# Decoder trunk on one core: weight halves kept in DRAM for the even layer only

## The chip, the cores and the metric

One Trainium2 chip, one of its cores. The metric is the time on the device of one launch, in microseconds (us). The kernel before took 2595.64 us in the median of three runs (2592.78 to 2598.08).

## The reference, cut to what matters

A hybrid decoder trunk takes one step for 1024 prompt tokens and 8 sample tokens, 1032 columns in all, with a model width of 1024 and everything in float32. It has two layers.

- Layer 0 (even) is an RMSNorm, one input projection of 1024 x 2560, sliding-window attention beside an RWKV-7 recurrence, an output projection, and a ConvFFN.
- Layer 1 (odd) is an RMSNorm, a gated chunk mixer, and a second ConvFFN. The mixer is `z = gelu(x W)`, split into u and v; v gets a LayerNorm and is mixed over chunks of 128 tokens; then `(u * mixed) W_out`.
- Each ConvFFN is `gelu(conv3(x W_gate)) * (x W_up)`, then `W_down`, with 2816 = 22 x 128 inner columns.

A float32 product is made of three matmuls: every operand is split into a high part `hi` (rounded to the float32r type) and a rest `lo = x - hi`, and `hi*hi + hi*lo + lo*hi` is summed (`mm3`, L288).

## The kernel before, in words

Activations lie transposed, 128 features on the partitions and tokens along the row. After the even mixer the 1032 tokens are in two halves (`HALVES`, L780): hA is chunk 0 with 512 tokens, and hB is chunks 1 and 2 with 256 and 264.

Weights come in slabs, 128 output columns by 1024 inputs. A global list `order` (L177 to L191) names every slab in the order of use. `wget` (L275) hands out the next slab and sees that the following ones are loaded, `LOOK2` = 3 slabs ahead in the layers' later parts. `wload` (L235) does the loading. From index `wfirst` on, the first slab of `gate0`, it counts as `late`. For each half j (128 x 512) of a slab:

- on the first visit, the raw half goes into a `raw` tile (a ring of `NRAW` = 3) by a DMA of 256 KB on SP's queue (L259); ACT copies it into `hi` (L285), and POOL computes `lo` (L286; for a few slabs it is DVE);
- if the slab will be asked for again (`more`), both parts are stored to DRAM as `wk`, 256 KB each, again on SP's queue (L263);
- on a later visit (`again`), both parts are loaded from there straight into the `w` tiles (L254), and nothing is split.

The `w` tiles are a ring of 18 in the late part (8 with tag `w`, 10 with tag `w2`), so four and a half slabs fit.

Late slabs that are asked for twice, once for hA and once for hB: gate and up, f = 0 to 7 in layer 0 and f = 0 to 5 in layer 1 (`gate_up`, L560); the last eight `down` slabs of either layer (`down`, L710, four slabs to a step: two steps for hA, then two for hB); and all slabs of `win_odd` and `wout_odd` (`odd_mix`, L1619). These are 24 + 20 + 24 = 68 slabs. The remaining gate and up slabs go through `pair` (L677), which builds combinations of weights (`wa`, `ws`) and touches each slab once. The even layer asks for each of its 28 slabs four times.

Around the gate and up steps of hB stands `combos` (L593): it loads the activations again (`ta`, `yA`, `yB` from `xnd`, L599) and forms differences of them on DVE, with splits on ACT, DVE and POOL, for the pairs that follow.

SP issues nearly all DMAs, in order. Engines work in program order; which order that is, a list scheduler decides at build time from simulated times and priorities. So the order in time differs from the order of the code.

Of the kernel before, what the change touches and what calls it, by code (L numbers as in the profile page):

```python
# [123 lines left out]
def trunk(ctx: ExitStack, tc: tile.TileContext, A, O):  # L124
# [12 lines left out]
    def nm(s):  # L137
        uid[0] += 1
        return f"{s}_{uid[0]}"
# [18 lines left out]
    def dram(shape, s, dt=F32):  # L158
        return dp.tile(shape, dt, tag=s, name=s)
# [17 lines left out]
    order = []  # L177
# [22 lines left out]
    def wtile(late):  # L200
        if late:
            wcount[0] += 1
        if late and (wcount[0] <= 4 * W2ONLY or wcount[0] % (NW + FBUFS["w2"]) >= NW):
            return wmore[0]("w2", 512, F32R)
        return wp.tile([P, 512], F32R, tag="w", name=nm("w"))
# [3 lines left out]
    def wfactor(name, f, i):  # L209

        if i == 0:
            wraw[name, f] = [stile("wa")[:, 0:512] for _ in range(4)]
            for k, t in enumerate(wraw[name, f]):
                SP.dma_start(out=t, in_=A[name][f + k // 2][:, k % 2 * 512:k % 2 * 512 + 512])
        r = wraw[name, f]
        if i == 0:
            return r[0]
        if i == 1:
            r.append(stile("ws", "g")[:, 0:512])
            DVE.tensor_tensor(out=r[4], in0=r[2], in1=r[3], op=ALU.add)  # L220
            return r[4]
        if i == 2:
            DVE.tensor_tensor(out=r[4], in0=r[4], in1=r[0], op=ALU.subtract)
            return r[4]
        if i == 3:
            return r[1]
        if i == 4:
            DVE.tensor_tensor(out=r[2], in0=r[0], in1=r[2], op=ALU.subtract)
            return r[2]
        if i == 5:  # L230
            DVE.tensor_tensor(out=r[4], in0=r[1], in1=r[4], op=ALU.subtract)
            return r[4]
        return r[3]

    def wload(i):  # L235


        late = i >= wfirst
        if late:
            look[0] = LOOK3 if len(order[i]) == 3 else LOOK2  # L240
        if len(order[i]) == 3:
            hi, lo = wtile(late), wtile(late)
            split(wfactor(*order[i]), hi, lo, POOL)
            wtiles[i] = tuple([x[:, k * P:(k + 1) * P] for k in range(4)] for x in (hi, lo))
            return
        name, m = order[i]
        again = order.index((name, m)) < i
        more = order.count((name, m)) > 1
        hi, lo = [], []
        for j in range(2):  # L250
            t = [wtile(late) for _ in range(2)]
            if again:
                for part in range(2):
                    SP.dma_start(out=t[part].bitcast(F32), in_=wkept[name, m, j, part])  # L254
                hi.append(t[0])
                lo.append(t[1])
                continue
            raw = wp.tile([P, 512], F32, tag="raw", name=nm("raw"), bufs=NRAW)
            SP.dma_start(out=raw, in_=A[name][m][:, j * 512:j * 512 + 512])  # L259
            split(raw, *t, DVE if SW[0] <= i - wfirst < SW[1] and i % SW[2] == 0 or i < SW[3] else POOL)  # L260
            for part in range(2 if more else 0):
                kept = wkept[name, m, j, part] = dram([P, 512], nm("wk"))
                SP.dma_start(out=kept, in_=t[part].bitcast(F32))  # L263
            hi.append(t[0])
            lo.append(t[1])
        wtiles[i] = ([hi[k // 4][:, (k % 4) * P:(k % 4 + 1) * P] for k in range(KD)],
                     [lo[k // 4][:, (k % 4) * P:(k % 4 + 1) * P] for k in range(KD)])
# [7 lines left out]
    def wget(*key):  # L275
        i = wpos[0]
        wpos[0] += 1
        assert order[i] == key, (order[i], key)
        while wnext[0] <= min(i + look[0], len(order) - 1):
            wload(wnext[0])  # L280
            wnext[0] += 1
        return wtiles.pop(i)

    def split(src, hi, lo, eng=None):
        ACT.activation(out=hi, in_=src, func=AF.Copy)  # L285
        (eng or DVE).tensor_tensor(out=lo, in0=src, in1=hi.bitcast(F32), op=ALU.subtract)  # L286
# [1533 lines left out]
```

## Time and profile before

| | us |
|---|---|
| median of 3 runs | 2595.64 |
| the profiled execution's own time | 2596.03 |
| its span (first to last instruction) | 2594.2 |

A profile's page lists the busy time of each engine over the span, the same in 40 slices, the DMA queues, the chain of work that ended last, the costliest groups of instructions, and the DMA issues with their time from issue to landing. PE is the matmul engine, ACT and DVE and POOL work on rows of 128 partitions, SP issues DMAs. "Idle before" an instruction is the time in which its engine stood still, and the releaser is what it waited for. In the table of windows each row is one stretch of the span, with the busy time of each engine, the granted clock of PE, the busy share of the DMA engines and the GB/s that they moved.

In the span, layer 0's gate and up steps begin in earnest at about 742 us, hB's at about 864 us; its last down steps are at 1440 to 1516 us. The odd mixer is at about 1520 to 1830 us, layer 1's gate and up steps follow to 1987 us, and its last down steps are at 2495 to 2566 us.

### The profile page before, as it was taken

The numbers are of one execution on the slowest core, as the hardware profiler recorded it, in microseconds if no ns is written. First come the engines' busy times: TensorE is split into PE (matmuls) and PEld (weight loads), VectorE is DVE, ScalarE is ACT, GpSimd is POOL, SyncE is SP. The second block draws the span as 40 slices with busy tenths as digits, with TensorE's granted clock in tenths as the row PEclk, the third lists the DMA queues.
The fourth block names the chain that finished last, engine by engine and source line by source line (L and its number), as shares of the span: only waits on it lengthen the run. The fifth ranks groups of instructions, "written<-read, shape, count | busy, mean of one in ns | idle before, by whom it ended". The sixth has DMA issues, their size and how long they took to land.

```text
span 2594.2 us, 49897 instructions
## 1 busy us (share of the span) xinstructions
PE 2450.8 (94%) x18508; PEld 2263.8 (87%) x18508; DVE 1600.0 (62%) x3471; ACT 982.8 (38%) x1937; POOL 863.2 (33%) x943
## 2 busy tenths in 40 slices
PE   6799998999889799999999899998999999999996
PEld 5688887888777699999999787988889999998986
DVE  5776859656864636766455476345576766655545
ACT  4444535434343334444411244443544444441110
POOL 1601113110434215555322344211534555542221
PEclk9889999998799899999999999999999999999998
DMA  8777657765499962223646789565995233264585
GB/s 310 269 235 215 212 182 239 239 220 161 157 328 326 351 227 99 98 103 123 227 132 211 280 271 314 185 207 162 329 357 201 97 105 120 85 208 147 187 282 167
DMA packets 330069, 542.89 MB, mean 209 GB/s; under 512 B 52769, under 2 KB 96353, under 8 KB 329825
## 3 DMA queue, kind: packets, MB, share of 16 engines
q1 hardware_dynamic: 329824, 539.70, 61.9%
q8 instruction: 145, 2.38, 0.4%
q14 instruction: 100, 0.81, 0.1%
HBM read 353.93 MB, written 183.00 MB: 207 GB/s over the span
## 4 chain that ended last, share of the span: by engine, by line
PE 77%; DVE 9%; DMA 6%; issue 3%; POOL 2%; ACT 2%; SPq 1%; DVEq 0%; POOLq 0%; ACTq 0%
PE l L289 17%; PE l L290 17%; PE l L291 17%; PE le L291 3%; PE le L289 3%; PE le L290 3%; PE m L291 2%; PE m L289 2%; PE m L290 2%; DMA w<-wk 2%; POOL w L286 1%; PE ch L1490 1%; PE ch L1493 1%; DMA raw<-in_win_even_dram 1%; PE pr L1380 1%
## 5 line engine op out<-in xcount | busy, mean ns | idle before, releaser
L286 POOL TENSOR_TENSOR w<-raw,w 128x512 fp32r<-128x512 f32 x228 | 310.8, 1373 | 603.1 <-ACT w L285 546.6
L289 PE MATMUL l<-xB,w 128*128 128x256 f32 (+2 forms) x1072 | 303.2, 286 | 18.7 <-DMA w<-wk 10.2
L285 ACT ACTIVATE w<-raw 128x512 fp32r<-128x512 f32 x248 | 153.4, 628 | 417.6 <-PE l L290 257.0
L289 PE MATMUL l<-xA,w 128*128 128x258 f32 (+1 forms) x896 | 301.8, 337 | 6.5 <-ACT w L285 5.9
L291 PE MATMUL l<-xA,w 128*128 128x258 f32 (+1 forms) x896 | 301.9, 337 | 3.5 <-POOL w L286 3.3
L291 PE MATMUL l<-xB,w 128*128 128x264 f32 (+2 forms) x1072 | 305.2, 286 | 0.0
L290 PE MATMUL l<-xB,w 128*128 128x264 f32 (+2 forms) x1072 | 304.8, 285 | 0.0
L290 PE MATMUL l<-xA,w 128*128 128x258 f32 (+1 forms) x896 | 301.6, 337 | 0.6 <-DVE xA L286 0.6
L289 PE MATMUL le<-xs,w 128*128 128x256 f32 (+1 forms) x896 | 270.1, 302 | 25.3 <-ACT w L285 19.5
L291 PE MATMUL le<-xs,w 128*128 128x256 f32 (+1 forms) x896 | 268.0, 300 | 9.7 <-POOL w L286 6.3
L290 PE MATMUL le<-xs,w 128*128 128x256 f32 (+1 forms) x896 | 265.3, 296 | 0.6 <-DVE xs L286 0.6
L289 PEld LDWEIGHTS l<-xB,w 128*128 128x128 f32 x1072 | 203.0, 191 | 20.5 <-ACT yA L285 10.6
L286 POOL TENSOR_TENSOR w<-wa,w 128x512 fp32r<-128x512 f32 x120 | 187.8, 1571 | 74.2 <-ACT w L285 65.4
L289 PEld LDWEIGHTS le<-xs,w 128*128 128x128 f32 x896 | 178.1, 199 | 37.9 <-ACT w L285 22.4
L290 PEld LDWEIGHTS l<-xB,w 128*128 128x128 f32 x1072 | 204.4, 191 | 0.2
L291 PEld LDWEIGHTS l<-xB,w 128*128 128x128 f32 x1072 | 204.1, 190 | 0.1
L291 PEld LDWEIGHTS le<-xs,w 128*128 128x128 f32 x896 | 177.6, 199 | 17.7 <-POOL w L286 8.1
L289 PEld LDWEIGHTS l<-xA,w 128*128 128x128 f32 x896 | 169.6, 189 | 25.6 <-ACT w L285 7.4
L291 PEld LDWEIGHTS l<-xA,w 128*128 128x128 f32 x896 | 169.5, 189 | 22.5 <-POOL w L286 4.6
L290 PEld LDWEIGHTS l<-xA,w 128*128 128x128 f32 x896 | 169.4, 189 | 18.0 <-DVE xA L286 0.7
L290 PEld LDWEIGHTS le<-xs,w 128*128 128x128 f32 x896 | 178.3, 199 | 4.6 <-issue 2.1
L725 DVE TENSOR_TENSOR yA<-yA,l 128x512 f32<-128x512 f32 x128 | 87.5, 687 | 149.7 <-PE l L291 149.7
(484 smaller groups left out, 6635.4 us busy)
## 6 DMA issues: line engine op xcount, KB each, us to landing
w<-wk SPq DMA_DIRECT2D x608, 256.0 KB, 4.1
wk<-w SPq DMA_DIRECT2D x384, 256.0 KB, 3.7
raw<-in_down_dram SPq DMA_DIRECT2D x88, 256.0 KB, 5.3
ta<-hd SPq DMA_DIRECT2D x36, 512.0 KB, 4.6
hd<-cb SPq DMA_DIRECT2D x30, 516.0 KB, 4.0
hd<-ub SPq DMA_DIRECT2D x30, 516.0 KB, 3.9
wa<-in_gate_dram SPq DMA_DIRECT2D x60, 256.0 KB, 2.9
wa<-in_up_dram SPq DMA_DIRECT2D x60, 256.0 KB, 2.6
```

Of the source, the lines that this page charges most:

```text
L285: ACT.activation(out=hi, in_=src, func=AF.Copy)
L286: (eng or DVE).tensor_tensor(out=lo, in0=src, in1=hi.bitcast(F32), op=ALU.subtract)
L289: PE.matmul(out, wh, xh, start=start, stop=False, **kw)
L290: PE.matmul(out, wh, xl, start=False, stop=False, **kw)
L291: return PE.matmul(out, wl, xh, start=False, stop=stop, **kw)
L725: DVE.tensor_tensor(out=yc, in0=yc, in1=ps[:, :n], op=ALU.add)
L1380: PE.matmul(pa[:, hp * 128:(hp + 1) * 128], BK[hp][s, e * 128:(e + 1) * 128], KR[hp][s, e * 128:(e + 1) * 128], start=True, stop=True)
L1490: PE.matmul(ps[:, hp * 128:(hp + 1) * 128], KR[hp][:, e * 128:(e + 1) * 128], Tc[:, hp * 128:(hp + 1) * 128], start=(hp == 0), stop=False, ...
L1493: PE.matmul(ps[r0:r0 + 64, h * 64:(h + 1) * 64], Av[e][:, h, r0:r0 + 64], UV[e][:, h * 64:(h + 1) * 64], start=False, stop=(h % 2 == 1), s ...
```

## The change

`again` and `more` are false for every late slab. The even layer goes on as before. Each late slab that is asked for twice is loaded raw and split on both visits, and is not stored in between.

```diff
         name, m = order[i]
-        again = order.index((name, m)) < i
-        more = order.count((name, m)) > 1
+        again = not late and order.index((name, m)) < i
+        more = not late and order.count((name, m)) > 1
         hi, lo = [], []
```

With 68 slabs of two halves and two parts, 272 stores `wk<-w` and 272 loads `w<-wk` go. In their place come 136 loads `raw<-in_...`, 136 ACT copies and 136 subtractions on POOL.

## Rows read from the trace of the kernel before

**Rows 1.** The page, busy time of the engines: us, share of the span, instructions.

```profile
PE 2450.8 (94%) x18508; PEld 2263.8 (87%) x18508; DVE 1600.0 (62%) x3471; ACT 982.8 (38%) x1937; POOL 863.2 (33%) x943
```

**Rows 2.** The page, the span in 40 slices, the busy share of each in tenths.

```profile
PE   6799998999889799999999899998999999999996
...
DMA  8777657765499962223646789565995233264585
```

**Rows 3.** The page, costliest groups: the split of raw halves on POOL and on ACT. After the bar: busy us, mean ns of one, idle before.

```profile
L286 POOL TENSOR_TENSOR w<-raw,w 128x512 fp32r<-128x512 f32 x228 | 310.8, 1373 | 603.1 <-ACT w L285 546.6
...
L285 ACT ACTIVATE w<-raw 128x512 fp32r<-128x512 f32 x248 | 153.4, 628 | 417.6 <-PE l L290 257.0
```

**Rows 4.** DMA issues over the whole span: count, KB each, median us from issue to landing.

```profile
w<-wk SPq DMA_DIRECT2D x608, 256.0 KB, 4.1
wk<-w SPq DMA_DIRECT2D x384, 256.0 KB, 3.7
raw<-in_down_dram SPq DMA_DIRECT2D x88, 256.0 KB, 5.3
...
raw<-in_gate_dram SPq DMA_DIRECT2D x28, 256.0 KB, 4.2
```

**Rows 5.** The table of windows: length, then PE, PEld, DVE, ACT and POOL busy with the number of instructions, PE's granted clock, DMA share, GB/s.

```profile
742.00:864.00 122.00, 109.47 (x539) 89.32 (x537) 69.64 (x123) 46.65 (x82) 52.94 (x56) 0.97 0.93 325
864.00:882.00 18.00, 5.51 (x27) 5.16 (x27) 13.16 (x13) 7.31 (x12) 6.27 (x6) 0.70 1.06 395
882.00:920.00 38.00, 35.33 (x283) 35.12 (x283) 20.04 (x34) 12.45 (x26) 5.67 (x8) 0.96 0.97 333
...
1840.00:1900.00 60.00, 60.00 (x292) 49.73 (x292) 43.73 (x85) 31.36 (x53) 38.23 (x41) 1.00 0.95 327
1440.00:1516.00 76.00, 65.96 (x421) 60.03 (x420) 47.17 (x96) 20.03 (x32) 17.88 (x13) 0.93 0.82 291
2495.00:2566.00 71.00, 65.78 (x426) 60.60 (x425) 31.92 (x68) 7.91 (x13) 6.57 (x7) 0.93 0.74 256
1620.00:1680.00 60.00, 60.00 (x494) 59.25 (x492) 23.08 (x34) 24.64 (x47) 9.34 (x8) 1.00 0.53 175
```

**Rows 6.** The timeline of PE: start us, us, instruction, and in brackets the idle time before it with its releaser.

```profile
831.36 0.50 PE L291 MATMUL l<-xA,w 128*128 128x512 f32 x1 [1.96 <-POOL w L286]
...
874.27 0.55 PE L289 MATMUL l<-xB,w 128*128 128x256 f32 x1 [10.16 <-DMA w<-wk]
...
906.06 0.39 PE L289 MATMUL l<-xB,w 128*128 128x256 f32 x1 [2.67 <-DVE gb L588]
...
1451.43 0.79 PE L289 MATMUL l<-gb,w 128*128 128x512 f32 x1 [3.72 <-ACT w L285]
...
1477.56 0.74 PE L291 MATMUL l<-cb,w 128*128 128x256 f32 x4 [3.57 <-DMA w<-wk]
...
2552.84 0.36 PE L289 MATMUL l<-gb,w 128*128 128x256 f32 x1 [1.77 <-DMA w<-wk]
```

**Rows 7.** The chain that ended last, in order of time: start us, us, what.

```profile
852.47 7.14 DMA wk<-w
...
859.68 5.24 DMA wk<-w
...
864.94 6.62 DMA yB<-xnd
...
1443.66 7.01 DMA raw<-in_down_dram
```

**Rows 8.** DMA issues of two stretches alone, 760 to 870 us (first row) and 1620 to 1690 us (second row): count, KB each, median us to landing.

```profile
wk<-w SPq DMA_DIRECT2D x50, 256.0 KB, 4.3
...
wk<-w SPq DMA_DIRECT2D x22, 256.0 KB, 2.4
```

**Rows 9.** The timelines of POOL (first row) and DVE at 897 to 903 us.

```profile
899.44 3.00 POOL L286 TENSOR_TENSOR yB<-t,yB 128x516 fp32r<-128x516 f32 x2
...
897.99 0.22 DVE L546 SCALAR_TENSOR_TENSOR gb<-st,vec,gb 128x8 f32<-128x8 f32 x1
...
899.27 0.75 DVE L543 SCALAR_TENSOR_TENSOR cb<-cb,vec 128x512 f32<-128x512 f32 x1
899.94 1.27 DVE L546 SCALAR_TENSOR_TENSOR cb<-st,vec,cb 128x8 f32<-128x8 f32 x1
901.13 1.86 DVE L543 SCALAR_TENSOR_TENSOR gb<-gb,vec 128x512 f32<-128x512 f32 x1
```

**Rows 10.** DVE at 900 to 1000 us, one group: the product that empties a PSUM bank in `gate_up`.

```profile
L588 DVE TENSOR_TENSOR cb<-cb,l 128x256 f32<-128x256 f32 x4 | 1.7, 418 | 0.8 <-ACT cb L586 0.8
```

## The prediction

> **What bounds the kernel now.** I read the busy times first: PE is busy 94% of the span, DVE 62, ACT 38, POOL 33 [rows 1]. PE bounds the whole, and an edit that changes no matmul can only give back or take PE's idle time and its lost clock. The slices (64.9 us each) then show where the DMA engines are full: the 12th to 14th (713 to 908 us), the 24th and 25th, the 29th and 30th and the 39th have 8 or 9 tenths. PE falls to 7 tenths in the 14th and to 8 in the 23rd, and keeps its 9 in the 29th and 30th [rows 2]. So I took windows of the late part [rows 5]. Idle time of PE is the length less its busy time: 12.5 us in hA's gate and up steps of layer 0 (742 to 864), 12.5 in the 18 us after them, 2.7 in 882 to 920, 10.0 in layer 0's last down steps, 5.2 in layer 1's. Two windows have none: 1840 to 1900, hA's gate and up of layer 1, and 1620 to 1680, in the odd mixer. The first of these is a warning: loads, splits and stores run there as at 742 to 864, the DMA engines are 0.95 busy, and PE stands still for 0.00 us. Full DMA engines alone cost nothing; it needs something that waits for one transfer.
>
> The timeline gives those places [rows 6]: 10.16 us at 874 on a load `w<-wk`, 3.72 at 1451 on an ACT split, 3.57 at 1477 and 1.77 at 2552 on `w<-wk`, 1.96 at 831 on a POOL split, 2.67 at 906 on DVE. The chain in order of time tells what is behind the first: two stores `wk<-w`, 7.14 and 5.24 us, stand on it one after the other, and only then the load `yB<-xnd` of 6.62 us whose data DVE needs before it comes to xB [rows 7]. And the ACT split at 1451 stood behind a raw load that took 7.01 us to land [rows 7], where the median over the span is 5.3 [rows 4].
>
> **The change part by part.** It takes 272 of 384 stores and 272 of 608 reloads out [rows 4] and puts 136 raw loads in: 408 transfers of 256 KB fewer, 107 MB. It adds 136 ACT copies of 0.628 us, 85 us, and 136 POOL subtractions of 1.373 us, 187 us [rows 3]. Spread over the span that takes POOL from 33% to 40% and ACT from 38% to 41%. Both have room; the question is place.
>
> *Second visits in general.* A slab of hB is 48 matmuls. At 60 us for 494 of them [rows 5] that is 5.8 us, against 2.7 us of POOL and 1.3 us of ACT for its two halves. Supply of raw halves: a ring of three, each held for its landing (4.2 us), ACT (0.63) and POOL (1.37), together 6.2 us [rows 3, 4]; so a half every 2.1 us and a slab every 4.1, under 5.8. The cover is PE's own work on a slab. If a landing took 7.01 us [rows 7] it would be 9.0 us for three, 6.0 per slab, and PE would wait 0.2 us per slab. In the odd mixer I therefore cost the second visits at 0; there is no idle time to win there. Bounds: 0 and +5 (two stalls as at 906).
>
> *hA of layer 0, 742 to 864.* 64 stores (16.8 MB of the 39.6 MB that 325 GB/s move in 122 us [rows 5]) go. Landings should fall from 4.3 us towards the 2.4 of a window at half the load [rows 8]. The order of the engines stays about the same, and 1840 to 1900 shows that such a stretch need not wait for stores at all. I take 3 of the 12.5 us: the 1.96 at 831 and about half as much elsewhere. Bounds: -12.5 and +3 (a changed order).
>
> *The start of hB, 864 to 882.* The two stores on the chain are 12.4 us [rows 7]. In place of one of them a raw load of 4.2 us [rows 4] may stand, so the load of `yB` comes some 8.2 us earlier. After that, while only hB's first chunk is there, PE needs a slab in 24 matmuls (2.9 us) and the raw ring gives one in 4.1: 1.2 us late per slab, for two slabs 2.4. The clock is 0.70 here for 5.51 us of matmuls [rows 5]; without the long stall 1.7 us of that comes back. Sum: -8.2 + 2.4 - 1.7 = -7.5. Bounds: -14.2 (all idle time and all of the clock), and +5 (four slabs late, no gain).
>
> *DVE and POOL side by side, in hB of both layers.* Here 32 and 24 subtractions come to POOL that were not there. What they do to DVE can be seen at 899 to 903 us [rows 9]: L546 takes 0.22 us alone and 1.27 while POOL subtracts, L543 0.75 and 1.86. The two POOL instructions cost DVE 2.2 us, and PE's wait of 2.67 us at 906 for L588 follows upon it [rows 6]. DVE is busy 33.2 of 56 us here [rows 5], so about every second new subtraction meets it. PE only feels it when four PSUM banks are full (4 x 2.9 = 11.6 us of cover). I take one more such wait, +2.7. Bounds: -2.7 (the wait at 906 goes, since `combos` starts earlier) and +21 (four in each layer).
>
> The Trainium skill has a rule for this, in "SBUF — State Buffer", section "Who interferes with whom": a DVE instruction with two inputs in SBUF and a GpSimd instruction that reads SBUF exclude each other for the whole instruction. The trace agrees in kind: L546 and L543, with two such inputs, are held, while L588, with one input in PSUM, keeps a mean of 418 ns [rows 10]. By the rule every meeting costs DVE up to a whole subtraction, and the sum below would be the second rival's.
>
> *Last down steps.* Four slabs to a step leave 2 of 18 `w` tiles over, so most of the next step's halves can only be split when the last matmuls of a step release tiles. For a step of hB I estimate what PE waits as 6.2 us (landing, ACT, POOL) less 2.9 us of matmuls on the halves already there: 3.3 us, twice per layer, 6.6. In layer 0 the two reload waits and what goes with them are 10.0 - 3.72 = 6.3 us now [rows 5, 6]: +0.3. The 3.72 at 1451 shrinks by 7.01 - 4.2 = 2.8. Of the clock (0.93 on 66 us, 4.6 us) I take 0.5 back. Sum -3.0; bounds -14.6 and +6 (landings of 7.01 us: 2 x 6.1 - 6.3). In layer 1 it is 6.6 against 5.2 us now: +1.4; bounds -9.8 and +7.
>
> *SP.* Its queue has 408 issues fewer. A raw load may hold it until a raw tile is free, as a reload held it until a `w` tile was free; I cost this at nothing, since the DMAs behind are the same.
>
> Sum: 0 - 3 - 7.5 + 2.7 - 3.0 + 1.4 = -9.4 us. Against the profiled execution's 2596.03 us that is 2586.6; its time is 0.4 us above the median of the runs, which is nothing here. I predict 2587.
>
> **The rivals.**
> 1. *Everything that waits for a weight transfer goes.* For it: 10.16 + 3.72 + 3.57 + 1.77 + 1.96 us of waits are weight waits [rows 6], and some 6 us of clock go with them: -27, 2569. Against it: in the down steps tiles, not transfers, are short.
> 2. *POOL holds DVE: slower.* In the stretches where `combos` runs, about 39 us in layer 0 and 24 in layer 1, two subtractions come per 5.8 us, 22 in all. If each two of them cost PE what the two at 899 did, that is 11 x 2.67 = 29 us, against 12 us of gains: +17, 2613. It decides once DVE's queue is more than 11.6 us behind, so that all four banks wait. For it: 2.67 us at 906 [rows 6, 9]. Against: in 1840 to 1900 POOL is busy 38 and DVE 44 of 60 us, and PE never waits [rows 5].
> 3. *The raw ring is too short in the down steps.* With landings of 7 us, +13 in both layers, and no more than 5 won elsewhere: 2604.
> 4. *Hidden anyway.* The stall at 874 is replaced by another of the same length, since hB's start hangs on the norm before it and its round trip through DRAM: 2595, within 3. For it: the 0.00 us at 1840 to 1900 in spite of a DMA share of 0.95 [rows 5].
>
> That the change does not do what it says I leave out: 272 + 112 and 272 + 336 give just the 384 and 608 of rows 4.
>
> **How the numbers follow.** Forecast (2581 to 2592) 0.42; rival 1 0.16; rival 4 0.22; rival 2 0.12; rival 3 0.08. About 0.2%, or 5 us, is what can be told from no change. Faster takes nine tenths of the forecast and rival 1: 0.53. Slower takes rivals 2 and 3 and a little of rival 4: 0.22. The rest, 0.25, is the same. The range of 8 in 10 leaves out the far ends of rivals 1 and 2: 2566 to 2608; the forecast's own is 2581 to 2592.
>
> **What would show it.** Right: at hB's start no store on the chain, and a wait of under 5 us in place of 10.16; DMA share at 742 to 864 near 0.55; waits for ACT or POOL `w` of 3 to 4 us at the down steps of hB; L543 and L546 more often above 1 us between 865 and 960. Wrong: PE waiting for L588 or L725 many times (rival 2), waits of 6 us and more for ACT `w` behind raw loads in the down steps (rival 3), or the same 10 us at hB's start with another releaser (rival 4). What would undo the whole sum is a schedule that puts other work of layer 0 elsewhere.

## The result: slower by 0.8%, and the profile after

The changed kernel takes 2619.06 us in the median of four runs (2615.42 to 2625.9), beside 2595.45 us of the kernel before (2592.78 to 2598.08). The ratio is 1.0081 [1.0059, 1.0103], 23.6 us more. The forecast was 2587, and 2619 lies outside its range. The profiled execution has a span of 2613.6 us against 2594.2: 19.4 us to explain.

The page of the kernel after: busy times, the slices, the groups that split weights, and the issues.

```profile
PE 2465.5 (94%) x18508; PEld 2275.2 (87%) x18508; DVE 1653.2 (63%) x3471; ACT 1060.0 (41%) x2073; POOL 1056.8 (40%) x1079
...
PE   6899998999899799999999899998989999999996
...
DMA  9876767765576742324643543224564233254444
...
L286 POOL TENSOR_TENSOR w<-raw,w 128x512 fp32r<-128x512 f32 x364 | 504.5, 1396 | 681.1 <-ACT w L285 579.4
L285 ACT ACTIVATE w<-raw 128x512 fp32r<-128x512 f32 x384 | 238.8, 629 | 554.3 <-PE l L290 355.6
...
w<-wk SPq DMA_DIRECT2D x336, 256.0 KB, 4.2
raw<-in_down_dram SPq DMA_DIRECT2D x120, 256.0 KB, 3.8
wk<-w SPq DMA_DIRECT2D x112, 256.0 KB, 3.4
```

Against [rows 1, 3, 4] the counts are those of the diff: 136 more splits on POOL and ACT, 272 fewer stores and 272 fewer reloads. POOL (40%) and ACT (41%) come out at the forecast shares. Two things do not. DVE executes the same 3471 instructions, and is busy 53.2 us longer. And PE executes the same 18508 matmuls and is busy 14.7 us longer; its idle time (span less busy) grows only from 143.4 to 148.1. So on balance three quarters of the 19.4 us are longer matmuls: the mean granted clock of the span is 0.967 before and 0.960 after. The share of 94% shows none of this.

To place the loss I counted PE's matmuls from the end of either trace in windows of 20 us, and noted when the same number was still to come. That gives, for each point of the work, how far a kernel is ahead or behind, good to a few us, since some matmul records are missing. The work that fills 720 to 840 us of the kernel before lies at 719.5 to 828.1 us in the one after, and so on. These are the windows of the same work, four stages, in the columns of [rows 5]; first the kernel before:

```profile
720.00:840.00 120.00, 109.17 (x584) 91.68 (x583) 72.45 (x137) 52.63 (x103) 49.94 (x66) 0.97 0.93 328
840.00:920.00 80.00, 61.65 (x396) 55.96 (x395) 46.26 (x71) 28.16 (x50) 21.96 (x29) 0.91 1.00 350
1440.00:1560.00 120.00, 109.65 (x657) 97.39 (x656) 81.14 (x161) 40.55 (x66) 45.41 (x35) 0.96 0.84 292
1880.00:1960.00 80.00, 78.33 (x514) 71.07 (x513) 63.58 (x113) 34.53 (x63) 31.43 (x34) 1.00 1.02 357
```

and the kernel after (719.5 answers to 720, 828.1 to 840, 1433.2 to 1440, 1883 to 1880):

```profile
1433.20:1561.40 128.20, 114.04 (x655) 101.69 (x654) 86.45 (x162) 51.60 (x85) 68.84 (x54) 0.91 0.50 165
828.10:913.80 85.70, 63.96 (x391) 57.12 (x390) 59.45 (x81) 39.11 (x71) 51.34 (x46) 0.84 0.68 219
719.50:828.10 108.60, 107.64 (x588) 91.73 (x588) 70.24 (x129) 53.43 (x101) 53.19 (x69) 1.00 0.74 244
1883.00:1980.00 97.00, 84.38 (x511) 76.11 (x512) 81.74 (x117) 46.74 (x85) 63.31 (x54) 0.93 0.68 222
```

- hA's gate and up steps of layer 0 gain 11.4 us: PE's idle time there falls from 10.8 to 1.0 us.
- hB's, of layer 0, lose 5.7 us: 3.4 of idle time and 2.3 of longer matmuls.
- The last down steps of layer 0 with the entry to the odd layer lose 8.2 us: 3.8 of idle time and 4.4 of longer matmuls.
- hB's gate and up steps of layer 1 lose 17.0 us. Idle time rises from 1.7 to 12.6 us, and 0.93 on 84.4 us of matmuls is another 5.9 us: 16.8 together. DVE works 18.2 us longer on the same work.

What is left over (920 to 1440: -0.6; 1560 to 1880: +1.6; after 1960: -0.2) is within the error of the method.

PE's timeline of the kernel after names the waits (columns as in [rows 6]):

```profile
859.80 0.58 PE L289 MATMUL l<-xB,w 128*128 128x256 f32 x1 [9.00 <-ACT xB L285]
...
892.92 0.39 PE L289 MATMUL l<-xB,w 128*128 128x256 f32 x1 [3.21 <-DVE gb L588]
...
1463.41 0.39 PE L289 MATMUL l<-cb,w 128*128 128x256 f32 x1 [2.75 <-ACT w L285]
...
1504.33 0.58 PE L289 MATMUL l<-ta,w 128*128 128x256 f32 x1 [4.32 <-DVE yB L725]
...
1945.88 0.38 PE L289 MATMUL l<-xB,w 128*128 128x256 f32 x1 [3.86 <-ACT cb L576]
...
1964.62 0.58 PE L289 MATMUL l<-xB,w 128*128 128x256 f32 x1 [3.95 <-ACT gb L576]
...
2542.63 0.62 PE L352 MATMUL pp<-cst,pp 128*128 128x128 f32 x4 [3.30 <-DVE pp L310]
...
2550.28 0.58 PE L289 MATMUL l<-ta,w 128*128 128x256 f32 x1 [4.54 <-DVE yB L725]
```

Of the waits for weights of [rows 6] one of 2.75 us is left. In their place PE waits for L588 and L725 on DVE and L576 on ACT, which empty PSUM (where matmuls leave their sums), and once for the norm's L310 on DVE. What makes DVE late is in the chain in order of time (start, us, what), at the entry to the odd layer and in layer 1's hB:

```profile
1495.20 1.18 DVE xA L286
1496.38 0.34 DVE yB L725
1496.72 3.06 DVE xA L286 x2
...
1500.43 0.60 DVE xA L286
...
1503.95 0.34 DVE yB L725
...
1947.40 1.78 DVE xc L616
1949.18 2.23 DVE ub L609
1951.41 1.14 DVE yA L286
1952.56 1.70 DVE t L614
...
1954.59 1.36 DVE t L614
...
1960.41 1.76 DVE cb L543
1962.17 1.16 DVE cb L546
...
1964.11 0.47 ACT gb L576
```

and beside it POOL's timeline:

```profile
1493.28 4.25 POOL L286 TENSOR_TENSOR w<-raw,w 128x512 fp32r<-128x512 f32 x3 [4.79 <-PE l L291]
...
1500.54 2.85 POOL L286 TENSOR_TENSOR w<-raw,w 128x512 fp32r<-128x512 f32 x2 [1.32 <-ACT w L285]
...
1948.59 1.73 POOL L286 TENSOR_TENSOR w<-raw,w 128x512 fp32r<-128x512 f32 x1
...
1951.43 3.97 POOL L286 TENSOR_TENSOR w<-raw,w 128x512 fp32r<-128x512 f32 x2
```

Two DVE instructions and POOL's work ahead of the wait at 1946, from their timelines:

```profile
1940.43 2.33 DVE L610 TENSOR_TENSOR ub<-yB,ub 128x1032 f32<-128x1032 f32 x1
...
1942.68 1.75 DVE L614 TENSOR_TENSOR t<-yB,yA 128x516 f32<-128x516 f32 x1
```

```profile
1940.39 3.50 POOL L286 TENSOR_TENSOR w<-raw,w 128x512 fp32r<-128x512 f32 x2
```

The same operation, `xA` on DVE, takes 0.60 us where it begins ahead of POOL's next subtraction (1500.43 and 1500.54), and 1.18 or 1.53 while POOL subtracts; `t` takes 1.36 to 1.70. At 1504 PE waits for the `yB` (L725) that stands behind these in DVE's order. At 1946 and 1965 it waits for ACT's L576. That stands in ACT's order behind work on what DVE makes: at 1946 behind splits of `ub` (L610) and `t`, at 1965 behind a gelu (L586) that needs L543 and L546. Not all of the delay at 1965 is the change's: from 1959 to 1963 POOL makes two of `combos`' own subtractions. The groups of DVE between 1880 and 1985 us (busy, mean ns) show the lengthening as a whole; before:

```profile
L614 DVE TENSOR_TENSOR t<-yB,yA 128x516 f32<-128x516 f32 x4 | 3.8, 962 | 1.2 <-POOL yB L286 1.2
L616 DVE TENSOR_TENSOR xc<-xc,ub 128x516 f32<-128x516 f32 x4 | 3.7, 962 | 0.0
```

and after:

```profile
L616 DVE TENSOR_TENSOR xc<-xc,ub 128x516 f32<-128x516 f32 x4 | 5.8, 1497 | 0.0
L614 DVE TENSOR_TENSOR t<-yB,yA 128x516 f32<-128x516 f32 x4 | 5.7, 1414 | 0.0
```

L588, with one input in PSUM, keeps its time: 426 ns before, 427 after over the span (128x264).

### The profile page after: what moved, and what is told of

Read it like the earlier page. It is cut to its first block, busy times and chain, and to the rows that moved or that the text cites. A ratio compares the mean times of both kernels' runs of the same rounds, so it can differ in the third digit from the quotient of the medians.

```text
span 2613.6 us, 49610 instructions
## 1 busy us (share of the span) xinstructions
PE 2465.5 (94%) x18508; PEld 2275.2 (87%) x18508; DVE 1653.2 (63%) x3471; ACT 1060.0 (41%) x2073; POOL 1056.8 (40%) x1079
## 4 chain that ended last, share of the span: by engine, by line
PE 78%; DVE 10%; DMA 6%; issue 2%; ACT 2%; POOL 1%; SPq 1%; DVEq 0%; ACTq 0%; POOLq 0%
PE l L289 17%; PE l L290 17%; PE l L291 17%; PE le L289 3%; PE le L291 3%; PE le L290 3%; PE m L291 2%; PE m L289 2%; PE m L290 2%; DMA w<-wk 1%; PE ch L1490 1%; DVE sq L325 1%; PE ch L1493 1%; POOL w L286 1%; PE pr L1380 1%
## 5 line engine op out<-in xcount | busy, mean ns | idle before, releaser
L286 POOL TENSOR_TENSOR w<-raw,w 128x512 fp32r<-128x512 f32 x364 | 504.5, 1396 | 681.1 <-ACT w L285 579.4
L285 ACT ACTIVATE w<-raw 128x512 fp32r<-128x512 f32 x384 | 238.8, 629 | 554.3 <-PE l L290 355.6
L286 POOL TENSOR_TENSOR w<-wa,w 128x512 fp32r<-128x512 f32 x120 | 187.5, 1568 | 64.3 <-ACT w L285 64.3
L286 POOL TENSOR_TENSOR w<-ws,w 128x512 fp32r<-128x512 f32 x90 | 129.9, 1443 | 141.3 <-ACT w L285 119.8
```

## The experiments

Three theories stood first. A: POOL's new subtractions hold DVE back (rival 2). B: the new ACT copies delay what ACT empties. C: the raw ring of three is too short (rival 3). Within A: A1, the subtraction blocks DVE since it reads SBUF (the memory that holds the tiles); A2, POOL's queue is merely longer, and what waits for POOL comes later. Each kernel's median, its ratio to the kernel before on the same chip, and the change in us of the four stages above (positive: slower than before; from one profiled execution each, by the same count of matmuls):

| kernel: how a second visit gets its parts | median | ratio [95%] | 720-840 | 840-920 | 1440-1560 | 1880-1960 |
|---|---|---|---|---|---|---|
| the changed kernel: ACT and POOL | 2619.06 | 1.0081 [1.0059, 1.0103] | -11 | +6 | +8 | +17 |
| e5: same, and the stores made all the same | 2617.73 | 1.0073 [1.0044, 1.0101] | +3 | +1 | +2 | +11 |
| e10: POOL in gate1/up1 and down0, else DVE | 2605.03 | 1.0018 [1.0003, 1.0033] | -11 | +2 | +1 | +14 |
| e12: POOL in down0, else DVE | 2602.62 | 1.0000 [0.9985, 1.0015] | -12 | +1 | +1 | +9 |
| e9: DVE in gate1/up1 and down0, else POOL | 2600.19 | 0.9985 [0.9967, 1.0004] | -12 | +10 | -7 | +11 |
| e11: POOL in gate1/up1, else DVE | 2592.63 | 0.9974 [0.9956, 0.9992] | -13 | +2 | -6 | +15 |
| e3: ACT and DVE | 2591.02 | 0.9973 [0.9955, 0.9991] | -13 | +3 | -5 | +10 |
| e6: ACT; `lo` kept in DRAM | 2593.97 | 0.9957 [0.9934, 0.9980] | -8 | +2 | -4 | +2 |
| e4: both parts loaded, no stores | 2582.09 | 0.9937 [0.9911, 0.9964] | -7 | -5 | -5 | +4 |
| e8: ACT and DVE, gate1/up1 kept as before | 2582.09 | 0.9919 [0.9891, 0.9946] | -12 | +1 | -8 | -1 |
| e7: ACT, and POOL writes zeros | 2582.46 | 0.9907 [0.9878, 0.9937] | -12 | -4 | +2 | +5 |
| e2: ACT twice, POOL nothing | 2572.19 | 0.9902 [0.9871, 0.9933] | -13 | -1 | -10 | +6 |

Four cautions. The list scheduler orders every kernel anew, so stages differ between kernels for reasons besides the edit. At 720 us, before the first edited visit, traces already differ by up to 8 us; stages can be compared better than sums. The kernel before took 2597 to 2602 us in the median beside e2 to e12, so the ratios are to be compared and not the medians. And one execution is not the median: the profiled ones lie 7 to 11 us under it in e3, e6 and e12, and 4 to 9 us over it in e2, e5 and e10.

e4, e6 and e8 are edits of the kernel before, the others of the changed one. In the cuts of code `...` stands for what is left out or as it was.

**e2, `lo` copied by ACT** (no POOL work on second visits; `lo` there is a copy and not the rest, so the sum of three matmuls is not the product):

```diff
+            if late and order.index((name, m)) < i:
+                for x in t:
+                    ACT.activation(out=x, in_=raw, func=AF.Copy)
+            else:
+                split(raw, *t, DVE if ... else POOL)
```

> On second visits of late slabs ACT copies the raw half into both w tiles, so lo is not the difference there; everything else is as in the changed kernel (2619 us). POOL is back at about 863 us busy, ACT rises to about 1145. Theory A (the new POOL subtractions hold DVE, so PSUM banks are emptied late): the loss in hB of layer 1 and in the last down steps of layer 0 goes, 2585 to 2595. Theory B (the new ACT copies stand in ACT's queue before the evictions): 85 us more of ACT make it worse, 2620 to 2640. Theory C (the ring of three raw tiles is too short): as the changed kernel, 2615 to 2622.

Ratio 0.9902: not only is the loss gone, it is a gain of 1%. ACT is busier than in any other kernel of the table (1124.6 us), so B falls; the loss is with POOL. C is only weakened by this run: the ring is the same, but a raw tile is held for two copies (1.3 us) in place of a copy and a subtraction (2.0). What speaks against C is that PE waits 2.75 us for a split of weights in the changed kernel's last down steps, where C wants 6 and more.

**e3, the subtraction on DVE**: `split(raw, *t, DVE if late and order.index((name, m)) < i or ... else POOL)`

> The subtraction of second visits goes to DVE instead of POOL, 136 of about 0.69 us. Theory A: DVE loses 0.69 us per half instead of up to 1.05, and not only where they meet; 2600 to 2615, with L543 and L614 back near 0.75 and 0.7 us in hB of layer 1. Theory B: as the changed kernel or worse. Theory C: as the changed kernel, 2615 to 2622.

Ratio 0.9973. DVE does 136 more instructions and the kernel is 1% faster than with them on POOL. Its groups at 1880 to 1985 us:

```profile
L614 DVE TENSOR_TENSOR t<-yB,yA 128x516 f32<-128x516 f32 x4 | 2.7, 685 | 0.0
L616 DVE TENSOR_TENSOR xc<-xc,ub 128x516 f32<-128x516 f32 x4 | 2.6, 684 | 0.0
```

The same `t` that takes 1414 ns in the changed kernel takes 685. For the work of the last stage (here 1859.5 to 1949.1 us):

```profile
1859.50:1949.10 89.60, 80.11 (x513) 73.03 (x512) 77.19 (x137) 47.93 (x86) 34.42 (x33) 0.94 0.72 239
```

DVE is busy 77.2 us with the 24 subtractions made by itself, 81.7 us in the changed kernel without them.

**e4, no stores and no splits**: a second visit loads both parts, always from the first late slab's place, so with other weights.

```diff
-        again = not late and order.index((name, m)) < i
-        more = not late and order.count((name, m)) > 1
+        again = order.index((name, m)) < i
+        more = order.count((name, m)) > 1 and i <= wfirst
...
-                    SP.dma_start(out=t[part].bitcast(F32), in_=wkept[name, m, j, part])
+                    SP.dma_start(out=t[part].bitcast(F32), in_=wkept[(*order[wfirst], j, part) if late else (name, m, j, part)])
```

> Late slabs are not stored, but for the first one; second visits reload two parts by DMA as before the change, always those of that first slab, so the products of second visits use other weights. It is the kernel before without 268 stores and with nothing else added. If the stores were what held hA and hB of layer 0 and the first of the last down steps: the gain of 12 + 9 us seen there without the losses, 2570 to 2585. If the stores were hidden: 2590 to 2597.

Ratio 0.9937: the stores are worth some 16 us. The reloads land in 4.1 us in the median, as before the change.

**e5, the stores made all the same**:

```diff
-        more = not late and order.count((name, m)) > 1
+        more = order.count((name, m)) > 1 and order.index((name, m)) == i or not late and order.count((name, m)) > 1
```

> The changed kernel with the 272 stores put back, which nobody reads; second visits load raw and split anew. Theory A or B: the losses of the changed kernel stay and the gain of hA of layer 0 and the down steps goes, 2630 to 2645. If the stores have no part in it: 2617 to 2622.

The stores cost 14 us in hA's stage of layer 0 (+3 against -11), and the end is the same as without them (2617.73 against 2619.06, intervals overlap). So the two prices do not add. The later stages are less slow here than in the changed kernel; why was not found.

**e7, POOL as busy without reading**: on a second visit ACT makes `hi`, and POOL fills the `lo` tile with zeros three times.

```diff
+            if late and order.index((name, m)) < i:
+                ACT.activation(out=t[0], in_=raw, func=AF.Copy)
+                for _ in range(3):
+                    POOL.memset(t[1].bitcast(F32), 0.0)
+            else:
+                split(raw, *t, DVE if ... else POOL)
```

> On second visits of late slabs POOL no longer subtracts: it fills the lo tile with zeros three times (a fill of 512 columns takes about 0.53 us in the trace of before, so 1.5 us or so per half, as long as the subtraction), after ACT has made hi. lo is zero there, everything else is as in the changed kernel. POOL writes but reads nothing. Theory A1 (a POOL instruction that reads SBUF holds DVE's two-input instructions): the losses go, 2572 to 2590. Theory A2 (POOL's own queue is the trouble: lo comes late, or the other POOL work stands behind it): POOL is as busy as in the changed kernel and it stays at 2610 to 2622.

The fills on the page, and `t` at 1880 to 1985 us (lines are 5 higher in this kernel):

```profile
L263 POOL MEMSET w<- 128x512 f32 x408 | 205.7, 525 | 115.1 <-PE l L296 100.3 <-PE l L295 5.0
```

```profile
L619 DVE TENSOR_TENSOR t<-yB,yA 128x516 f32<-128x516 f32 x4 | 2.6, 686 | 0.0
```

POOL is busy 1063.7 us here and 1056.8 in the changed kernel, and DVE 1598.4, as before the change (1600.0). The ratio is 0.9907. So over the kernel it is not POOL's time but its reading of SBUF: A1, not A2. The fills differ in one more thing, which no run takes apart: they wait for no raw half and no copy, and hold no raw tile. One stage is an exception. At 1440 to 1560 us e7 is at +2, near e12's +1, and e2 at -10; there POOL's residual additions (`yA`, L474 in the changed kernel) stand in its queue behind the fills, so A2 has a share in that place. And there the fills do hold DVE, in an instruction with one input (a TENSOR_SCALAR on 128x4, L310 in this kernel and L305 in the kernel before, where its mean is 171 ns). On the chain it takes 2.73 us beside a row of fills; the chain first, then POOL's timeline:

```profile
1480.65 2.73 DVE pp L310
```

```profile
1477.70 5.64 POOL L263 MEMSET w<- 128x512 f32 x12
```

What only writes is harmless to `t`, then, and not to every DVE instruction.

**e6, `lo` kept and `hi` made anew** (one store on the first visit, one reload and one raw load on the second, no subtraction):

```diff
+            if late and seen:
+                ACT.activation(out=t[0], in_=raw, func=AF.Copy)
+                SP.dma_start(out=t[1].bitcast(F32), in_=wkept[name, m, j, 1])
+            else:
+                split(...)
...
+            for part in (() if not more or late and seen else (1,) if late else (0, 1)):
```

> A version that keeps half: the first visit stores lo alone, a second visit loads the raw half, makes hi anew on ACT and reloads lo. No subtraction is added to POOL, 136 of 272 stores go. Between the kernel before and the one without stores (2582): theory A gives 2580 to 2592. If it is the raw ring or ACT that costs: above 2600.

Ratio 0.9957. With half of the stores left, and no subtraction, the kernel gains about half of what e7 gains.

**e9, e10, e11, e12, which engine in which place.** In e9 DVE makes `lo` in gate1/up1 and in down0 (40 of 136 halves) and POOL elsewhere; e10 is its mirror image; e11 and e12 leave POOL one place each.

```diff
e9   DVE if late and order.index((name, m)) < i and name in ("gate1", "up1", "down0") or ...
e10  DVE if late and order.index((name, m)) < i and name not in ("gate1", "up1", "down0") or ...
e11  DVE if late and order.index((name, m)) < i and name not in ("gate1", "up1") or ...
e12  DVE if late and order.index((name, m)) < i and name not in ("down0",) or ...
```

> The changed kernel, but with the subtraction on DVE in second visits of gate and up of layer 1 and of the last down steps of layer 0 only (40 halves); the other 96 stay on POOL. Theory A with its place (POOL costs where DVE is nearly full and empties PSUM: the two stretches where the changed kernel loses 15 and 16 us): 2588 to 2600. If POOL's subtractions cost everywhere alike: 40 of 136 of the 28 us between POOL and DVE, 2610 to 2614.

> The changed kernel in which POOL makes the rest of the second visits only in gate1, up1 and down0 (40 of 136 halves); DVE makes the other 96. It is the mirror image of the run that had DVE in these places and came to 2600. Theory 1, that the loss is made in these two places by POOL's reading of SBUF: near the changed kernel, 2611 to 2620. Theory 2, that it grows with the number of POOL subtractions wherever they stand (187 us of them cost 28 us over the kernel with DVE alone, 2591): 40/136 of that, 2599, 2594 to 2603. Theory 3, that what a schedule built anew happens to be decides: anything from 2582 to 2620, and not the sum of the two runs with one place each.

> POOL makes the rest only in gate1 and up1 (24 of 136 halves), DVE everywhere else. Theory 1: the loss of some 15 us that the changed kernel has in hB's gate and up steps of layer 1 comes back beside DVE alone: 2591 + 5 to 15 = 2596 to 2606. Theory 2: 24/136 of 28 us: 2596, 2592 to 2600. In both, DVE's operations with two inputs in SBUF (t, xc) take 1.4 us and more in layer 1's hB and 0.7 to 0.95 us elsewhere.

> POOL makes the rest only in the last down slabs of layer 0 (16 of 136 halves), DVE everywhere else. Theory 1: the loss of some 16 us between layer 0's last down steps and the odd mixer comes back: 2591 + 5 to 16 = 2596 to 2607, with DVE's operations in the entry of the odd layer stretched. Theory 2: 16/136 of 28 us: 2594, 2590 to 2598.

Taking POOL out of the 40 halves gives back 0.0096 of the ratio, 25 us (e9 against the changed kernel). Putting it into them alone costs 0.0045, 12 us (e10 against e3); down0 costs 0.0027 of that and gate1/up1 0.0001, with intervals of about 0.0025 on such a difference. So theory 1 as I put it, that these places carry the loss alone, falls: the 96 other halves cost 3 us when DVE has the 40 (e9 against e3), and 16 when POOL has them too (changed kernel against e10). Theory 2 falls with the same 3 us: by number 96 of 136 would cost 20 of the 28. In e11 `t` is lengthened as in the changed kernel, though DVE makes all the other subtractions:

```profile
L616 DVE TENSOR_TENSOR xc<-xc,ub 128x516 f32<-128x516 f32 x4 | 5.9, 1503 | 0.0
L614 DVE TENSOR_TENSOR t<-yB,yA 128x516 f32<-128x516 f32 x4 | 5.6, 1412 | 0.0
```

and its last stage is at +15 against +10 of e3; in the median of the kernel that place made no difference (0.0001). Of the changed kernel's +17 there, then, 2 to 6 remain without any subtraction (e6, e4, e7, e2), some 5 more come with 24 subtractions on DVE (+9 to +11), and 0 to 7 more with POOL making them (+11 in e5, +14, +15 and +17). That is rough, from one execution each. Why the prices of the places do not add up to 28 us (changed kernel less e3) stays open. A part of it is the stage at 1440 to 1560, where the changed kernel is at +8 and e10 and e12, with the same POOL work in down0, at +1. Theory 3, that the order built anew makes a part of it, is not excluded by any run here.

**e8, a kernel that beats both**: DVE subtracts on second visits, and gate1/up1 are stored and reloaded as before the change.

```diff
+        anew = late and name not in ("gate1", "up1")
+        again = not anew and order.index((name, m)) < i
+        more = not anew and order.count((name, m)) > 1
...
+            split(raw, *t, DVE if late and order.index((name, m)) < i or ... else POOL)
```

> A candidate: second visits are split anew with the subtraction on DVE, except gate and up of layer 1, which are kept in DRAM as before the change. With all second visits on DVE (2591) some 10 us were lost in hB of layer 1, where DVE makes the combinations as well; without that loss 2578 to 2585. If the loss there came with the stores' absence and not with DVE's work: 2588 to 2594.

2582.09 us, 0.9919: 0.8% less than before. It keeps the gain in layer 0 and loses nothing at 1880 to 1960, where PE idled only 1.7 us before the change, with the DMA engines full, so that nothing was to be had.

## Why the prediction was wrong

- **The step that failed is "DVE and POOL side by side, in hB of both layers", +2.7.** Layer 1's hB alone lost 17 us, inside the term's upper bound of +21. What POOL does to DVE was sized nearly right: half of 24 subtractions at 1.1 us each is 13 us, and DVE took 18.2 longer. What DVE's delay does to PE was not. I let four PSUM banks cover it and allowed one more wait like the one at 906. The window shows 10.9 us of new idle time, and 5.9 us of lost clock, which the term did not contain at all. Nor is all of it POOL holding DVE: e3 loses 10 us there with the subtractions on DVE, and e6, e4, e7 and e2 lose 2 to 6 with none, which stays unexplained; the term put both at nothing. What I held against rival 2, the stretch at 1840 to 1900 without a wait, is hA's, where DVE has none of `combos`' work in its queue.
- The Trainium skill's rule ("SBUF — State Buffer", section "Who interferes with whom") excludes a DVE instruction with two SBUF inputs from running beside a GpSimd instruction that reads SBUF, and says that one which only writes does not contend. The runs agree on both halves: `t` takes 1412 ns in the mean with POOL's subtractions in that stage (e11) and 686 with fills (e7). I had said that by the rule the sum would be rival 2's. The time came out near it, though not only in rival 2's places.
- **Last down steps of layer 0, -3.0**: +8.2, the second step that failed. I looked there for weights only. Without POOL's new work in that place the sign is right (-10 in e2, -5 in e3). The entry to the odd layer puts the norm's DVE work with two SBUF inputs (`xA`, L286, and `sq`, L325) in the same 100 us, and the term had no line for it. Layer 1: +1.4 foretold, about +2 found between 2480 and 2560 us, and that is luck: I had 6.6 us of waits for splits of weights there, and PE has none; its waits of 3.30 and 4.54 us are for DVE's L310 and L725.
- **The start of hB, -7.5**: the third; hB's gate and up steps of layer 0 lost 5.7 us. No store `wk<-w` is on the chain any more, as foretold, but a wait of 9.00 us stands where 10.16 stood, now on `xB`. That is rival 4's mechanism in this place, hB's start hanging on the norm and its round trip through DRAM: `xB` is split from `xl`, which is loaded from `xnd`, and on the chain that leads on to the wait at 893 are 3.82 us of storing `xnd` and 6.20 us of loading it. The wait stays in e2, e3, e7 and e8 too (8.22, 8.35, 7.65 and 8.24 us).
- **hA of layer 0, -3**: -11.4, close to its lower bound of -12.5. The sign and the cause (stores) are shown by e5, where the stores come back and the stage goes to +3; the size was too timid. The DMA share at 742 to 864 us is 0.69, not 0.55.
- **Second visits in general, 0; SP, 0**: right. The odd mixer (1560 to 1880) is at +1.6.
- **Rivals.** Rival 2 came true, 2613 against 2619, and I gave it 0.12. Its number has luck in it: a part of the loss lies at the entry to the odd layer, where rival 2 had none, and a part of layer 1's hB is there without POOL. Rival 3's waits of 6 us and more for splits in the down steps do not occur. Rival 1's gain is there in size: without POOL's work on second visits (e2) the kernel is at 0.9902, 2570 of 2595.5, and rival 1 said 2569, although the wait at hB's start, which rival 1 had going, stayed. The gains that I halved and the loss that I made small were both real, and they were priced in separate terms although they meet in one kernel.

## What to carry to other kernels

Before work goes to an engine with idle time, look at what its instructions do to the neighbours while they run: here 24 subtractions on POOL cost DVE 18.2 us, and cost it 13.6 when DVE made them itself (e3). Saving transfers pays only in the stage where something waits for one; where PE already runs without waits, leave the stage alone, as e8 does. And when a wait on a PE-bound path is priced, price the clock after it too.

## What was not expected of the hardware

- On balance the clock took more than the waits: of 19.4 us of span, 4.7 are idle time of PE and 14.7 longer matmuls. That is so because hA's stage gave idle time back; in the three stages that lost, idle time grew by 18.2 us and matmuls by 12.8. In layer 1's hB the mean granted clock fell from 1.00 (2.4 GHz throughout) to 0.93, so part of the stretch ran at the lower of the two levels, 1.2 GHz. Before it stood PE's waits of up to 3.95 us, where the longest had been 1.46.
- DVE instructions with both inputs in SBUF are held by POOL's subtractions, narrow ones too: L546, on 8 columns, takes 1.16 us at 1962, and 0.22 alone [rows 9]. L588 and L725, with one input in PSUM, keep their mean to a few ns. POOL's fills, for the same POOL time, leave DVE at 1598.4 us, but they too held a TENSOR_SCALAR with one input (2.73 us in e7).
- 272 stores of 256 KB cost 16 us where nothing else is late (e4) and nothing measurable in a kernel whose DVE is late (e5 against the changed kernel).
